# A two-layer retention and neighbourhood-attention transformer on one core: first stage with its loads put in another order, fewer unread products, and the decay tables and strips later

## The chip, the cores and the metric

One core of one Trainium2 chip. The core has TensorE (PE), VectorE (DVE), ScalarE (ACT), GpSimd (POOL) and SyncE (SP), and 16 DMA engines. Each engine works through its own row of instructions in order, and waits on semaphores for the others; DMAs are issued from the rows of SP, ACT and POOL. The metric is the device time of one execution in microseconds (us), lower is better; several runs are given by their median.

## The reference, cut to what matters

```python
for i in range(DEPTH):                       # 2 layers, D_MODEL 1024, 256 tokens x and 256 tokens ctx
    mod = (silu_c @ ada_w[i] + ada_b[i])[:, None, :]
    mod_c = silu_cc @ ada_w[i] + ada_b[i]
    sh1, sc1, g1, sh2, sc2, g2 = jnp.split(mod, 6, axis=-1)
    ...
    h = x * (1.0 + sc1) + sh1
    hc = ctx * (1.0 + sc1c) + sh1c
    if i % N_MIXERS == 0:
        y, yc = retention_mixer(h, hc, ret_w_in[j], ret_w_o[j], ret_decay[j], ang_row, ang_col, not last)
    else:
        y, yc = neighbourhood_mixer(h, hc, nat_w_in[j], nat_w_o[j], nat_rpb[j], not last)
    x = layer_norm(DN_ALPHA * x + g1 * y, ln_g[i, 0], ln_b[i, 0])
    h = x * (1.0 + sc2) + sh2
    x = layer_norm(DN_ALPHA * x + g2 * sq_relu_mlp(h, mlp_w1[i], mlp_w2[i]), ln_g[i, 1], ln_b[i, 1])
    ...                                      # ctx likewise, in the first layer
```

The retention layer projects `h @ w_in` to q, k, v and a gate for 4 heads, and weighs its scores with powers of a decay, `log_gamma = -exp(ret_decay)`, in both directions. All of it is float32.

## The kernel before, in words

Each float32 product is made of three products of a rounded format: every operand is split into a high part (a cast on ACT) and a low part (raw minus high, on DVE), and `mm3` adds high x high, high x low and low x high in PSUM. A weight therefore goes through a DMA into a raw tile, a cast `hi<-raw` and a subtraction `lo<-raw,hi` before TensorE reads it. Raw tiles come from a pool of four buffers, high and low parts from pools of five. Nearly every instruction has L89 as its line, since a helper issues it; tiles are told apart by name.

The change lies in the first stage (lines 888 to 953), which makes the modulation and the q and v projections of the first head. It goes in four quarters `i` of 256 of the 1024 rows that are contracted. A quarter needs

- its tokens: 256 columns of x and of ctx, one DMA each into `R` (`RR`)
- its columns of `ada_w`: four DMAs into `rawq`, in two pairs of arena slots used in turn (`AQ`)
- its rows of the q weights and the v weights: two DMAs into `raw`

and does the following. TensorE sums `ada_w` against silu(c) into `pada` (`quarter_sums`), turns the row of sums to columns (`quarter_columns`, `mod`), transposes two chunks of tokens (`chunk`, `pt`), and makes q products (`quarter_q`, into `pq`) and v products (`quarter_v`, into `pv`) of both chunks. ACT and DVE apply the modulation to one half of a chunk each (`aff<-pt,mod`), split the result (`hTh`, `hTl`), and split the weights. The sums, transposes and casts of quarter i+1 stand between the products of quarter i.

Ahead of the first useful product, and in gaps between the first sums, TensorE makes products of a constant tile, `still`, which nobody reads (`turn_over(n)`: n calls, each two instructions in the records). At the very end of the kernel it makes forty more, `px`, that nobody reads either.

The decays take a path of their own. `strip_tables` loads `lgn` (`ret_decay`) and a table of distances `dt`; ACT takes the exponential of `lgn`, POOL makes four more tables of `dt`. `make_strip(h)` makes the strip of head h of them: four exponentials on ACT and five operations on DVE. The masked scores read the strips later. `ln_rows` and `cst1` are other small loads of this stage.

In this stage the rows of PE, ACT and DVE hold the program's order (`on=True`), as SP's does throughout. Elsewhere a scheduler sets the order of those engines. After the stage, for head 0, the q's are rotated, v is evacuated, and `proj_T` makes k.

Of the kernel before, what the change touches and what calls it, by code (L numbers as in the profile page):

```python
# [10 lines left out]
F32 = mybir.dt.float32  # L11
F32R = mybir.dt.float32r
# [97 lines left out]
def kernel(  # L110
# [139 lines left out]
    units = []  # L250
    taken = [0]
    pending = []

# [18 lines left out]
    def load():  # L272

        src, k, ncol = specs[len(units)]
        raw = rawp.tile([P, k, ncol], F32, tag="raw", name=nm("raw"))
        sp.dma_start(out=raw[:], in_=src.rearrange("(k p) n -> p k n", p=P))
        hi = hip.tile([P, k, ncol], F32R, tag="hi", name=nm("hi"))
        lo = lop.tile([P, k, ncol], F32R, tag="lo", name=nm("lo"))
        units.append((hi, lo))

        def high(i):
            act.copy(out=hi[:, i], in_=raw[:, i])

        def low(i):
            dve.tensor_sub(out=lo[:, i], in0=raw[:, i], in1=hi[:, i].bitcast(F32))

        return high, low

# [18 lines left out]
    cst1 = cpool.tile([P, CONSTS.shape[1] - NC0], F32, tag="cst1", name="cst1")  # L307
    crow = scr("crow")[:, :P]
    sp.dma_start(out=crow[0:8, :], in_=c.rearrange("a (k p) -> (a k) p", p=P))
    act.dma_start(out=crow[8:16, :], in_=c_ctx.rearrange("(k p) -> k p", p=P))  # L310
    act.dma_start(out=crow[16:32, :], in_=ada_b[0][0 : 2 * D].rearrange("(r p) -> r p", p=P))
    act.dma_start(out=cst0[:], in_=consts[:, 0:NC0])

# [445 lines left out]
    def strip_tables():  # L759
# [7 lines left out]

        dt = slot(S_VL, [P, 5, 384], F32, "dt")
        sp.dma_start(out=dt[:, 0], in_=dist)
# [117 lines left out]

    quarter_x(0, act)
    raws = ada_quarter_load(0, AQ[0])
    wq_parts, wv_parts = load(), load()  # L890
    raws1 = quarter_loads(1)
    for e in (act, dve, pe):
        e.on = True
    pr = bank("pada")
    turn_over(3)
    first_columns()
    turn_over(4)
    quarter_sums(pr, raws, 0, range(0, 4))
    pts = [chunk_kinds(k) for k in range(2)]
    turn_over(1)  # L900
    quarter_sums(pr, raws, 0, range(4, KC))
    turn_over(2)
    quarter_sums(pr, raws, 1, range(0, 4))
    turn_over(2)
    quarter_sums(pr, raws, 1, range(4, KC))
    row = quarter_row(pr)
    turn_over(1)
    quarter_columns(pr, row, 0)
    turn_over(2)
    (qhigh, qlow), (vhigh, vlow) = wq_parts, wv_parts  # L910
    qhigh(0)
    modulate_kinds(0, pts[0], lambda: qlow(0))
    vhigh(0)
# [7 lines left out]
    pv = [bank("pv") for _ in range(4)]  # L921
    sp.dma_start(out=cst1[:], in_=consts[:, NC0:])

    for i in range(4):
        k = 2 * i
        wq, wv = take(2, 0)
        if i < 3:
            wq_parts, wv_parts = load(), load()
        if i == 0:
            rows = ln_rows()  # L930
            tabs = strip_tables()
        quarter_q(k, 0, wq)
        if i == 0:
            quarter_v(k, 0, wv)
            quarter_q(k + 1, 1, wq)
            quarter_v(k + 1, 1, wv, range(2))
        if i < 3:
            pr, row = quarter_rows(i + 1, raws)
        if i:
# [24 lines left out]
    act.on = dve.on = False  # L964
# [51 lines left out]
    for h in range(RH):  # L1016
# [3 lines left out]
        if h == 0:  # L1020
# [951 lines left out]
    flat = hTh[:].rearrange("p k t -> p (k t)")  # L1972
    px = bank("px")
    for d, m_, n_, far in (
        (0, P, 512, 0), (16, P, 512, 0), (32, P, 512, 0), (64, P, 512, 0), (112, P, 512, 0),
        (4, P, 512, 0), (0, 64, 512, 0), (0, P, 512, 1), (0, P, 256, 0), (64, P, 256, 0),
    ):
        src = hTl[:].rearrange("p k t -> p (k t)") if far else flat
        for _ in range(4):
            pe.matmul(  # L1980
                px[:m_, :n_], lhsT=src[:, 2048 + d : 2048 + d + m_], rhs=flat[:, :n_], start=True, stop=True
            )
    last_norm(0, 0, quarter(0), *m0)
# [49 lines left out]
```

## Time and profile before

| | |
|---|---|
| runs | 1236.78, 1232.69, 1232.66 us; median 1232.69 |
| profiled execution | 1234.7 us, its span 1232.9 us |
| mean granted clock of TensorE, profiled execution | 0.996 of full |
| busy: DVE, ACT, POOL | 811.1, 480.1, 170.8 us |
| moved by DMA | 194.30 MB, 158 GB/s over the span |
| first unread product | at 1.48 us |
| exponential of the decays | at 25.22 us |

A row of a timeline gives the start, the length, the engine, the operation with tile out<-in, and in brackets the idle time ahead of it on its engine with what released it. "hi<-raw" is a cast of weights, "lo<-raw,hi" the low part. A row of windows gives a stretch of the span, and for each engine how long it was busy with how many instructions, then the clock that TensorE was granted (1.00 is full) and the share and rate of the DMA engines.

### The profile page before, as it was taken

The numbers are of one execution on the slowest core, as the hardware profiler recorded it, in microseconds if no ns is written. First come the engines' busy times: TensorE is split into PE (matmuls) and PEld (weight loads), VectorE is DVE, ScalarE is ACT, GpSimd is POOL, SyncE is SP. The second block draws the span as 40 slices with busy tenths as digits, with TensorE's granted clock in tenths as the row PEclk, the third lists the DMA queues.
The fourth block names the chain that finished last, engine by engine and source line by source line (L and its number), as shares of the span: only waits on it lengthen the run. The fifth ranks groups of instructions, "written<-read, shape, count | busy, mean of one in ns | idle before, by whom it ended". The sixth has DMA issues, their size and how long they took to land.

```text
span 1232.9 us, 18106 instructions
## 1 busy us (share of the span) xinstructions
PE 1212.4 (98%) x7148; PEld 1013.4 (82%) x7148; DVE 811.1 (66%) x1265; ACT 480.1 (39%) x804; POOL 170.8 (14%) x203
## 2 busy tenths in 40 slices
PE   8999999999999999999999999999999989999999
PEld 6767788888888888888888888888887868999887
DVE  2598857777585476667766664467575677776445
ACT  2552221323223245442113341256465655565331
POOL 1103501420340140000120000231111100000002
PEclk9999999999999999999999999999999999999999
DMA  8756443375553224326656657335346543565660
GB/s 286 242 192 208 130 144 107 114 251 124 148 152 106 76 67 137 110 92 206 195 166 211 193 187 236 98 102 173 86 137 178 174 130 119 180 206 185 228 191 36
DMA packets 140213, 194.30 MB, mean 158 GB/s; under 512 B 22424, under 2 KB 83920, under 8 KB 140128
## 3 DMA queue, kind: packets, MB, share of 16 engines
q1 hardware_dynamic: 135328, 180.79, 47.1%
q0 software_dynamic: 3296, 9.49, 3.0%
q10 hardware_dynamic: 1504, 2.86, 0.7%
q8 instruction: 56, 0.92, 0.3%
q14 instruction: 29, 0.24, 0.1%
HBM read 188.28 MB, written 5.75 MB: 157 GB/s over the span
## 4 chain that ended last, share of the span: by engine, by line
PE 86%; DVE 5%; ACT 4%; DMA 3%; issue 2%; POOL 1%; SPq 0%; ACTq 0%; DVEq 0%; POOLq 0%
PE p L89 42%; PE pq L89 7%; PE pw L89 6%; PE pv L89 6%; PE pg L89 6%; PE pn L89 4%; PE pnv L89 3%; PE po L89 2%; PE pada L89 2%; ACT s L89 2%; DVE lo L89 1%; PE pS L89 1%; PE ppt L89 1%; PE pnw L89 1%; ACT hi L89 1%
## 5 line engine op out<-in xcount | busy, mean ns | idle before, releaser
L89 DVE TENSOR_TENSOR lo<-raw,hi 128x1024 fp32r<-128x1024 f32 (+1 forms) x235 | 277.5, 1192 | 162.4 <-ACT hi L89 162.0
L89 ACT CAST hi<-raw 128x1024 fp32r<-128x1024 f32 (+1 forms) x235 | 234.9, 1011 | 351.7 <-PE p L89 189.0
L89 PE MATMUL p<-hi,hid 128*128 128x512 f32 (+1 forms) x832 | 242.5, 374 | 0.0
L89 PEld LDWEIGHTS p<-hi,hid 128*128 128x128 f32 x832 | 152.2, 188 | 28.8 <-issue 1.2
L89 PE MATMUL p<-hTh,lo 128*128 128x256 f32 (+1 forms) x512 | 169.6, 331 | 0.8 <-DVE lo L89 0.8
L89 PE MATMUL p<-hTh,hi 128*128 128x256 f32 (+1 forms) x512 | 170.0, 332 | 0.0
L89 PE MATMUL p<-hTl,hi 128*128 128x256 f32 (+1 forms) x512 | 169.4, 331 | 0.0
L89 PE MATMUL p<-lo,hid 128*128 128x512 f32 (+1 forms) x416 | 155.4, 373 | 0.0
L89 POOL TENSOR_TENSOR R<-R,acc 128x512 f32<-128x512 f32 x40 | 66.8, 1680 | 299.1 <-DVE acc L89 299.1
L89 PEld LDWEIGHTS p<-hTh,lo 128*128 128x128 f32 x512 | 98.1, 192 | 9.8 <-DVE lo L89 1.0
L89 PEld LDWEIGHTS p<-hTh,hi 128*128 128x128 f32 x512 | 98.0, 192 | 9.5 <-issue 0.8
L89 PEld LDWEIGHTS p<-hTl,hi 128*128 128x128 f32 x512 | 98.1, 192 | 8.6
L89 DVE SCALAR_TENSOR_TENSOR acc<-rawa,scol,acc 128x1024 f32<-128x1024 f32 x49 | 62.2, 1282 | 42.9 <-DMA rawa<-in_ada_w_dram 42.8
L89 PEld LDWEIGHTS p<-lo,hid 128*128 128x128 f32 x416 | 78.4, 189 | 13.4
L89 DVE SCALAR_TENSOR_TENSOR strips<-rawa,scol,strips 128x512 f32<-128x512 f32 x84 | 70.1, 885 | 1.5 <-DMA rawa<-in_ada_w_dram 1.5
L89 ACT CAST hid<-r 128x256 fp32r<-128x256 f32 (+1 forms) x64 | 32.0, 500 | 82.7 <-DVE r L89 82.7
L89 ACT ACTIVATE s<-s,mn 128x512 f32<-128x512 f32 x64 | 45.5, 712 | 32.0 <-DVE mn L89 32.0
L89 DVE TENSOR_TENSOR hid<-r,hid 128x256 fp32r<-128x256 f32 (+1 forms) x64 | 34.6, 541 | 29.4 <-ACT hid L89 29.2
L89 PE MATMUL pw<-hi,oh 128*128 128x512 f32 x128 | 51.2, 400 | 0.0
L89 PE MATMUL pg<-hi,hTh 128*128 128x512 f32 x128 | 51.0, 398 | 0.0
L89 PE MATMUL pg<-lo,hTh 128*128 128x512 f32 x128 | 50.2, 392 | 0.4 <-DVE lo L89 0.4
L89 PE MATMUL pv<-hi,hTh 128*128 128x512 f32 x128 | 50.4, 394 | 0.0
(208 smaller groups left out, 2237.8 us busy)
## 6 DMA issues: line engine op xcount, KB each, us to landing
raw<-in_mlp_w_dram SPq DMA_DIRECT2D x128, 512.0 KB
rawa<-in_ada_w_dram SPq DMA_DIRECT2D x80, 512.0 KB
raw<-in_ret_w_in_dram SPq DMA_DIRECT2D x46, 512.0 KB
raw<-in_nat_w_in_dram SPq DMA_DIRECT2D x24, 512.0 KB
rawq<-in_ada_w_dram SPq DMA_DIRECT2D x16, 512.0 KB
raw<-in_ret_w_o_dram SPq DMA_DIRECT2D x16, 512.0 KB
bias<-rpb_rows POOLq DMA_DIRECT2D x16, 256.0 KB, 4.4
raw<-in_nat_w_o_dram SPq DMA_DIRECT2D x8, 512.0 KB
```

The lines of the kernel that those rows point to most:

```text
L89: r = f(*args, **kwargs)
```

## The change

- `load()` issues only the DMA; the high and low tiles are taken when the casts begin (`begin()`). All loads of quarters 0 and 1 are issued up front, those of quarter i+2 at the head of quarter i.
- The `ada_w` of quarter 0 is issued on SP ahead of quarter 0's tokens; these go from ACT's queue to SP's. The first constants go to the front of ACT's queue.
- `turn_over` goes from 15 calls (3, 4, 1, 2, 2, 1, 2) to 10 (5, 2, 1, 1, 1); the first two transposed chunks come behind the columns; the first cast of q weights stands in `modulate_kinds` between the two parts.
- `ln_rows`, `cst1` and `strip_tables` go from quarter 0 to quarter 1, behind the loads of quarter 3.
- `dt` goes from an arena slot to a tile of the constants' pool.
- The strips of heads 0 and 1 are made at the end of quarters 2 and 3, those of heads 2 and 3 after the first `proj_T`.
- The scaling of the residual `RR` by ALPHA, two DVE operations in quarter 3, becomes two ACT operations behind the first `proj_T` in the code; since ACT's order is the scheduler's there, it can put them where it finds room.
- The forty products `px` at the end are gone.

```diff
     def load():
-        src, k, ncol = specs[len(units)]
+        src, k, ncol = specs[loaded[0]]
+        loaded[0] += 1
         raw = rawp.tile([P, k, ncol], F32, tag="raw", name=nm("raw"))
         sp.dma_start(out=raw[:], in_=src.rearrange("(k p) n -> p k n", p=P))
-        hi = hip.tile([P, k, ncol], F32R, tag="hi", name=nm("hi"))
-        lo = lop.tile([P, k, ncol], F32R, tag="lo", name=nm("lo"))
-        units.append((hi, lo))
...
+        def begin():
+            hi = hip.tile([P, k, ncol], F32R, tag="hi", name=nm("hi"))
+            lo = lop.tile([P, k, ncol], F32R, tag="lo", name=nm("lo"))
+            units.append((hi, lo))
...
-        dt = slot(S_VL, [P, 5, 384], F32, "dt")
+        dt = cpool.tile([P, 2, D], F32, tag="G", name=nm("dt"))
+        dt = dt[:].rearrange("p a n -> p (a n)")[:, :1920].rearrange("p (k n) -> p k n", k=5)
...
-    quarter_x(0, act)
     raws = ada_quarter_load(0, AQ[0])
-    wq_parts, wv_parts = load(), load()
+    quarter_x(0, sp)
+    loads = [(load(), load())]
     raws1 = quarter_loads(1)
+    loads.append((load(), load()))
...
-    turn_over(3)
+    turn_over(5)
     first_columns()
-    turn_over(4)
-    quarter_sums(pr, raws, 0, range(0, 4))
-    pts = [chunk_kinds(k) for k in range(2)]
+    turn_over(2)
+    quarter_sums(pr, raws, 0, range(0, KC))
     turn_over(1)
-    quarter_sums(pr, raws, 0, range(4, KC))
-    turn_over(2)
     quarter_sums(pr, raws, 1, range(0, 4))
-    turn_over(2)
+    turn_over(1)
     quarter_sums(pr, raws, 1, range(4, KC))
     row = quarter_row(pr)
     turn_over(1)
     quarter_columns(pr, row, 0)
-    turn_over(2)
...
-    sp.dma_start(out=cst1[:], in_=consts[:, NC0:])
     for i in range(4):
         k = 2 * i
         wq, wv = take(2, 0)
+        if i < 2:
+            raws2 = quarter_loads(i + 2)
+            loads.append((load(), load()))
+        if i == 1:
+            rows = ln_rows()
+            sp.dma_start(out=cst1[:], in_=consts[:, NC0:])
+            tabs = strip_tables()
         if i < 3:
-            wq_parts, wv_parts = load(), load()
-        if i == 0:
-            rows = ln_rows()
-            tabs = strip_tables()
+            wq_parts, wv_parts = (f() for f in loads[i + 1])
...
-            if i < 2:
-                raws = quarter_loads(i + 2)
         else:
             ln_columns(rows)
             take(0, 3)
-            for a in range(2):
-                dve.tensor_scalar_mul(out=RR[a][:], in0=RR[a][:], scalar1=ALPHA)
...
-        for h in ((), (0,), (1,), (2, 3))[i]:
-            make_strip(h, *tabs)
+        if i > 1:
+            make_strip(i - 2, *tabs)
...
             proj_T(qkh[:, 2:4], qkl[:, 2:4], True)
+            for i in (2, 3):
+                make_strip(i, *tabs)
+            for a in range(2):
+                act.mul(out=RR[a][:], in_=RR[a][:], mul=ALPHA)
...
-    px = bank("px")
```

In the rows that follow, numbers behind a name only tell apart tiles of the same use.

On SP, before, the load of the decays `lgn` stands behind the constants and the q and v weights (`raw`) of quarter 1, and ahead of the loads of quarter 2:

```order
L89 DMA rawq_136<-in_ada_w_dram 128x4x256
L89 DMA rawq_137<-in_ada_w_dram 128x4x256
L89 DMA cst_82<-in_consts_dram 128x136
L89 DMA raw_239<-in_ret_w_in_dram 128x2x256
L89 DMA raw_243<-in_ret_w_in_dram 128x2x512
L89 DMA lgn<-in_ret_decay_dram 128x8
L89 DMA dt_255<-in_dist_dram 128x384
```

After, it stands behind the `ada_w` (`rawq_357`, `rawq_358`) and the weights of quarter 3:

```order
L89 DMA rawq_357<-in_ada_w_dram 128x4x256
L89 DMA rawq_358<-in_ada_w_dram 128x4x256
L89 DMA raw_363<-in_ret_w_in_dram 128x2x256
L89 DMA raw_365<-in_ret_w_in_dram 128x2x512
L89 DMA cst_82<-in_consts_dram 128x136
L89 DMA lgn<-in_ret_decay_dram 128x8
L89 DMA dt_376<-in_dist_dram 128x384
```

The load passes all the loads of quarters 2 and 3 on this queue.

On ACT, before, the exponential `lgn<-lgn` and its table load stand between the modulation of the first two chunks (`hTh`, `aff_225`) and that of chunk 2 (`aff_334`):

```order
L89 ACTIVATE hTh<-pt_171,mod_96 128x256
L89 ACTIVATE aff_225<-pt_172,mod_96 128x256
L89 CAST hi_132<-raw_130 128x512
L89 DMA rows_247<-in_ln_g_dram 32x128
L89 DMA rows_247<-in_ln_b_dram 32x128
L89 ACT_TABLE_LOAD
L89 ACTIVATE lgn<-lgn 128x8
L89 ACTIVATE aff_334<-pt_326,mod_96 128x256
L89 CAST hTh<-aff_334 128x512
L89 CAST hi_241<-raw_239 128x256 x2
```

After, they stand between the casts of quarter 1's v weights (`raw_140`) and the modulation of chunk 4 (`aff_447`), the first of quarter 2, whose q weights are `raw_245`:

```order
L89 ACTIVATE aff_346<-pt_341,mod_96 128x256
L89 CAST hTh<-aff_346 128x512
L89 CAST hi_251<-raw_140 128x512 x2
L89 DMA rows_367<-in_ln_g_dram 32x128
L89 DMA rows_367<-in_ln_b_dram 32x128
L89 ACT_TABLE_LOAD
L89 ACTIVATE lgn<-lgn 128x8
L89 ACTIVATE aff_447<-pt_439,mod_96 128x256
L89 CAST hTh<-aff_447 128x512
L89 CAST hi_382<-raw_245 128x256 x2
```

So the exponential has moved by one quarter, from ahead of chunk 2 to ahead of chunk 4.

On ACT, before, the last casts of the stage, those of quarter 3, follow one another with the modulation of chunks 6 and 7 between them:

```order
L89 ACTIVATE aff_571<-pt_563,mod_96 128x256
L89 CAST hTh<-aff_571 128x512
L89 CAST hi_504<-raw_502 128x256 x2
L89 ACTIVATE aff_591<-pt_586,mod_96 128x256
L89 CAST hTh<-aff_591 128x512
L89 CAST hi_508<-raw_506 128x512 x2
L89 ACTIVATE e_612<-dt_255,lgn 128x384
```

After, the two scalings of the residual, `R_100` (x) and `R_101` (ctx), stand among them:

```order
L89 ACTIVATE aff_553<-pt_545,mod_96 128x256
L89 CAST hTh<-aff_553 128x512
L89 CAST hi_488<-raw_363 128x256 x2
L89 ACTIVATE R_100<-R_100 128x2048
L89 ACTIVATE aff_573<-pt_568,mod_96 128x256
L89 ACTIVATE R_101<-R_101 128x2048
L89 CAST hTh<-aff_573 128x512
L89 CAST hi_490<-raw_365 128x512 x2
L89 ACTIVATE e_594<-dt_376,lgn 128x384
```

Both have moved ahead of the cast of chunk 7 and of quarter 3's v weights (`raw_365`).

More of the change, by code (lines that the diff above doesn't have):

```diff
@@ L251 @@
     taken = [0]
+    loaded = [0]
     pending = []
@@ L272, in load, with high, low @@
     def load():
-        src, k, ncol = specs[len(units)]
+        src, k, ncol = specs[loaded[0]]
+        loaded[0] += 1
         raw = rawp.tile([P, k, ncol], F32, tag="raw", name=nm("raw"))
         sp.dma_start(out=raw[:], in_=src.rearrange("(k p) n -> p k n", p=P))
-        hi = hip.tile([P, k, ncol], F32R, tag="hi", name=nm("hi"))
-        lo = lop.tile([P, k, ncol], F32R, tag="lo", name=nm("lo"))
-        units.append((hi, lo))
[L281 to L287, printed above, removed]
+        def begin():
+            hi = hip.tile([P, k, ncol], F32R, tag="hi", name=nm("hi"))
+            lo = lop.tile([P, k, ncol], F32R, tag="lo", name=nm("lo"))
+            units.append((hi, lo))
+            def high(i):
+                act.copy(out=hi[:, i], in_=raw[:, i])
+            def low(i):
+                dve.tensor_sub(out=lo[:, i], in0=raw[:, i], in1=hi[:, i].bitcast(F32))
+            return high, low
+        return begin
     def lows(n=100):
@@ L308 @@
     crow = scr("crow")[:, :P]
+    act.dma_start(out=cst0[:], in_=consts[:, 0:NC0])
     sp.dma_start(out=crow[0:8, :], in_=c.rearrange("a (k p) -> (a k) p", p=P))
@@ L311 @@
     act.dma_start(out=crow[16:32, :], in_=ada_b[0][0 : 2 * D].rearrange("(r p) -> r p", p=P))
-    act.dma_start(out=cst0[:], in_=consts[:, 0:NC0])
     def cv(name, p0=0, p1=P):
@@ L908 @@
     quarter_columns(pr, row, 0)
-    turn_over(2)
-    (qhigh, qlow), (vhigh, vlow) = wq_parts, wv_parts
-    qhigh(0)
-    modulate_kinds(0, pts[0], lambda: qlow(0))
+    pts = [chunk_kinds(k) for k in range(2)]
+    (qhigh, qlow), (vhigh, vlow) = (f() for f in loads[0])
+    modulate_kinds(0, pts[0], lambda: (qhigh(0), qlow(0)))
     vhigh(0)
@@ L938 @@
             pr, row = quarter_rows(i + 1, raws)
+            raws = raws2
         if i:
@@ L1971 @@
             mm2b(1, 1, u, held[2 * (u - 14) + 1], i)
-    flat = hTh[:].rearrange("p k t -> p (k t)")
-    px = bank("px")
[L1974 to L1982, printed above, removed]
     last_norm(0, 0, quarter(0), *m0)
```

## The prediction

> **What bounds the kernel now.** I read the page first. Its first line gives the span, its second the busy time of each engine, and the chain that ended last names who sets the end.
>
> ```profile
> span 1232.9 us, 18106 instructions
> PE 1212.4 (98%) x7148; PEld 1013.4 (82%) x7148; DVE 811.1 (66%) x1265; ACT 480.1 (39%) x804; POOL 170.8 (14%) x203
> PE 86%; DVE 5%; ACT 4%; DMA 3%; issue 2%; POOL 1%; SPq 0%; ACTq 0%; DVEq 0%; POOLq 0%
> ```
>
> TensorE is busy 98% of the span, so a stage can get faster only where TensorE does work that nobody reads or waits, and any new wait of TensorE counts in full. Next I read the timeline of TensorE through the first stage and into the next; columns are start, busy time of the row, engine, operation, tile out<-in, and in brackets the idle time ahead with its releaser.
>
> ```profile
> 1.48 2.93 PE L89 MATMUL pq<-still 128*128 128x256 f32 x6 [1.48 <-DVE still L89]
> 18.58 0.70 PE L89 MATMUL pq<-hTh,hi 128*128 128x512 f32 x2
> 35.64 0.64 PE L89 MATMUL pada<-rawq,cT 128*32 128x128 f32 x16 [0.46 <-DMA rawq<-in_ada_w_dram]
> 44.58 0.62 PE L89 MATMUL pq<-hTh,hi 128*128 128x512 f32 x2
> 48.26 0.40 PE L89 MATMUL pv<-lo,hTh 128*128 128x512 f32 x1
> 58.30 0.50 PE L89 MATMUL pv<-lo,hTh 128*128 128x512 f32 x1 [0.31 <-DVE lo L89]
> 80.12 0.50 PE L89 MATMUL pg<-lo,hTh 128*128 128x512 f32 x1 [0.45 <-DVE lo L89]
> 81.58 0.64 PE L89 MATMUL pada<-rawa,cT 128*32 128x256 f32 x8 [0.49 <-DMA rawa<-in_ada_w_dram]
> ```
>
> The first product that counts starts at 18.58. The later waits are under 0.5 us each: the front costs time, the rest of the stage almost none. What feeds the stage is in the windows; columns are the window, its length, busy time of PE, PEld, DVE, ACT and POOL with instruction counts, granted clock, DMA share and GB/s.
>
> ```profile
> 0.00:4.00 4.00, 2.52 (x6) 1.85 (x6) 0.54 (x2) 0.53 (x1) 0.41 (x6) 1.00 0.35 97
> 4.00:20.00 16.00, 13.19 (x106) 8.78 (x105) 3.10 (x11) 3.37 (x8) 0.00 (x0) 1.00 1.10 356
> 20.00:30.00 10.00, 9.92 (x102) 8.06 (x103) 4.18 (x10) 2.94 (x5) 4.18 (x3) 1.00 0.78 244
> 30.00:45.00 15.00, 14.00 (x122) 10.80 (x121) 6.70 (x15) 6.75 (x14) 2.68 (x5) 1.00 1.07 351
> ```
>
> The DMA engines run at about 350 GB/s, except in the ten microseconds from 20, where loads wait for their issue. What they carry, from the DMA issues of the first 45 us:
>
> ```profile
> rawq<-in_ada_w_dram SPq DMA_DIRECT2D x16, 512.0 KB
> raw<-in_ret_w_in_dram SPq DMA_DIRECT2D x4, 256.0 KB
> raw<-in_ret_w_in_dram SPq DMA_DIRECT2D x5, 512.0 KB
> R<-in_x_dram SPq DMA_DIRECT2D x3, 256.0 KB
> R<-in_ctx_dram SPq DMA_DIRECT2D x3, 256.0 KB
> ```
>
> A quarter is two token loads (0.524 MB), four ada loads (2.097) and two weight loads (0.262 and 0.524): 3.41 MB. The two pieces of the constants are 0.07 MB each by their shapes.
>
> **The change part by part.** *Front and loads (gain).* Five of 15 unread calls go, and ada precedes the tokens. What ends the front afterwards is one quarter with one constants piece, or 3.48 MB: an estimate at 356 GB/s from zero is 9.8 us, and with a landing lag of some 2 to 2.7 (below) and two casts about 13, against 18.58. That lead of some 5 us isn't kept whole, because ada of quarter 2 comes next. Before, 6.97 MB (two quarters, constants) plus the 0.20 of the distance table and 2.62 of tokens and ada stand ahead of the sums at 35.64: 9.79 MB. By 30 us some 8.5 MB had moved (the first three windows: 0.39, 5.70 and 2.44). The other 1.3 MB at 351 take 3.6 us: 33.6, so landing lags by 2.0. After, 9.53 MB stand there; the loads are issued as slots come free, so the rate can stay at 351: 20 + (9.53 - 6.1)/0.351 = 29.8, landed at 31.8. That is 3.8 us earlier. TensorE would then reach the product of quarter 2, now at 44.58, at about 40.7.
>
> *The decay load (loss).* The load of the decays goes on SP from behind quarter 1 to behind quarter 3. ScalarE's row is in program order, so its exp on that load stands ahead of the modulation and casts of chunk 4.
>
> ```profile
> 18.55 0.34 SPq L89 DMA_DIRECT2D lgn<-in_ret_decay_dram  x1
> 25.22 0.21 ACT L89 ACTIVATE lgn<-lgn 128x8 f32<-128x8 f32 x1 [1.67 <-DMA lgn<-in_ret_decay_dram]
> 40.94 0.56 ACT L89 ACTIVATE aff<-pt,mod 128x256 f32<-128x256 f32 x1 [5.38 <-DVE aff L89]
> 42.06 0.71 ACT L89 CAST hi<-raw 128x256 fp32r<-128x256 f32 x2
> 45.90 1.29 DVE L89 TENSOR_TENSOR lo<-raw,hi 128x512 fp32r<-128x512 f32 x2
> ```
>
> Before, the exp waits 1.67 us at 25.22, when ScalarE has little to do. Its 6.97 MB are through at 20 + 0.87/0.351 = 22.5, a lag of 2.7. After, four quarters and both constants, 13.8 MB, are ahead of it: 20 + 7.7/0.351 = 42.0, and with lags of 2.0 to 2.7 it lands at 44.0 to 44.7; I take 44.3. The exp ends 0.2 later. From modulation (40.94) to the first cast of quarter 2's q weights (half of the 0.71 from 42.06) are 1.5 us: its product starts at 46.0, 1.4 after 44.58. TensorE, there at 40.7, idles 5.3 us. From modulation to the first low part of the v weights (45.90 plus half of 1.29) are 5.6 us, so the second v product comes at 50.1 instead of 48.26: **+1.9** (1.6 to 2.3). This holds gain and loss together: the lead is spent waiting. The queue behind the exp is ScalarE's modulation, high parts and, through them, VectorE's low parts; TensorE waits for all.
>
> *Clock after that gap.* Two places of the trace show what follows idle time, each as a window and the next:
>
> ```profile
> 467.50:470.95 3.45, 1.44 (x10) 1.15 (x10) 1.21 (x3) 3.13 (x5) 0.00 (x0) 1.00 0.08 25
> 470.95:474.37 3.42, 3.31 (x15) 3.31 (x16) 3.24 (x8) 2.80 (x6) 0.00 (x0) 0.50 0.52 153
> 1010.26:1013.67 3.41, 0.58 (x26) 0.31 (x15) 1.92 (x6) 3.34 (x9) 0.00 (x0) 1.00 0.19 67
> 1013.67:1017.08 3.41, 3.41 (x40) 2.93 (x41) 3.01 (x6) 0.62 (x2) 0.00 (x0) 0.50 0.02 5
> ```
>
> A window with 2.0 of 3.45 us idle is followed by 3.4 us at half clock, and so is one with 2.8 idle. So 5.3 us idle brings at least one such stretch: 1.7 us of work lost, of which some 0.5 lies beside the wait for low parts: **+1.2** (0 to 2.9: none that shows, or two stretches with the same cover).
>
> *Scaling the residual (loss).* It leaves VectorE's row of quarter 3 for ScalarE's, as two instructions of 128x2048. They stand between the casts of quarter 3's q weights and its v weights, on both sides of the modulation of chunk 7. No ScalarE row has that size; the nearest are:
>
> ```profile
> 55.70 0.56 ACT L89 ACTIVATE aff<-pt,mod 128x256 f32<-128x256 f32 x1 [1.27 <-DVE aff L89]
> L89 ACT CAST hi<-raw 128x1024 fp32r<-128x1024 f32 x217 | 226.3, 1051 | 346.5 <-PE p L89 189.0 <-PE pg L89 49.7 <-PE pw L89 41.6
> L89 ACT CAST hi<-raw 128x512 fp32r<-128x512 f32 x10 | 5.8, 616 | 0.0
> L89 ACT ACTIVATE xn<-R,nmr,rstd 128x1024 f32<-128x1024 f32 x4 | 5.0, 1245 | 8.2 <-DVE nmr L89 8.2
> ```
>
> From 616 to 1051 ns for 512 columns more, another 1024 columns make 1.92 us. Twice 1051 or 1245 give 2.10 and 2.49. I take 1.92, since a longer instruction pays its start once: 3.84 for both, of which the 1.27 idle ahead of 55.70 takes part. The rest, 2.6, pushes the casts of the v weights, and TensorE already waits 0.31 for their low part at 58.30: **+2.6** (2.5 to 3.7). A gap of that length again precedes half clock in the rows above, but with its own low parts late behind it: **+1.0** (0 to 1.7).
>
> *VectorE (gain).* Two strips of five operations and the scaling leave its row.
>
> ```profile
> 64.88 1.22 DVE L89 TENSOR_SCALAR R<-R 128x2048 f32<-128x2048 f32 x1
> ```
>
> Two of 1.22 and ten strip operations come later or go; only the small waits at 80.12 and 81.58 can shrink: **-0.5** (0 to -0.9). The strips come after the first k projection, beside TensorE's work.
>
> *The unread products at the end.*
>
> ```profile
> 1223.65 5.40 SPq L89 DMA_DIRECT2D out_dram<-xn  x5
> 1227.51 1.55 SPq L89 DMA_DIRECT2D out_dram<-xn  x3
> 1229.01 1.11 PE L89 MATMUL px<-hTh 128*128 128x256 f32 x8
> ```
>
> TensorE's unread products end at 1230.1, the issue of the stores at 1229.1, and the span at 1232.9; the stores' landing sets the end, so: **0** (0 to -0.5, if the products delayed the stores' issue at all; the difference of their ends, 1.0, bounds it, and I take half). Of the rest, the first constants on ScalarE's queue and the transposes behind the columns cost nothing, as the bytes of quarter 0 set the front. The distance table comes on SP right behind the decays, and GpSimd makes four tables of it:
>
> ```profile
> L89 POOL TENSOR_SCALAR dt<-dt 128x384 f32<-128x384 f32 x4 | 5.7, 1435 | 24.9 <-DMA dt<-in_dist_dram 24.7
> ```
>
> From about 45 they take until 51. The first strip stands in ScalarE's row behind the v casts of quarter 3, later than 56, so that is hidden; nothing else waits on GpSimd there.
>
> *Sum.* 1.9 + 1.2 + 2.6 + 1.0 - 0.5 + 0 = +6.2. The profiled execution took 1234.7 us, 1.8 over its span; the median of the runs shown is 1232.69, so the sum gives 1240.9 on the profiled execution and **1238.9** on the median. The bounds of the sum are 1.6 + 0 + 2.5 + 0 - 1.4 = +2.7 and 2.3 + 2.9 + 3.7 + 1.7 = +10.6. As the ends are hardly met together, I take half the distance to each: 1237.1 to 1241.1 is the forecast's own range.
>
> [...] In the trace 2.0 and 2.8 us of idle time within one window of 3.4 us were enough for a half-clock window. [...]
>
> **The rivals.** Half a per cent, about what a measurement of this kernel can tell from no change, is 6.2 us: faster is below 1226.5, slower above 1238.9.
>
> *Only the long gap drops the clock* (0.16). The gap of 2.6 us is a wait between products, not a whole idle window: v's first product, q's two low products and others lie within it. For it: 2.6 us spread over two windows leaves each over half busy. Against: 467.50 has 1.44 of 3.45 us busy and was followed by half clock. The sum loses 1.0: 1237.9. [...]
>
> *The decay load lands in time* (0.14; no change). If the loads of quarter 3 run ahead, or the small load overtakes larger ones on free DMA engines, the exp has its data by 40.7 and the lead isn't spent: -3.8 in place of +1.9 and +1.2, with 2.6 + 1.0 - 0.5 left, -0.7: 1232.0. It decides at one number, the landing at 40.7 or before. Against: 7.7 MB from 20 at 351 GB/s takes until 42.0 without any lag, so the rate would have to be 373 GB/s or more. For: the window from 4 to 20 had 356 with a slow start in front.
>
> *The scaling hides too* (0.06). If, besides, ScalarE reaches it earlier, as its lead grows with TensorE's, 3.6 of loss go: -4.3, 1228.4. Against: TensorE already waits at 58.30 with only 1.27 idle on ScalarE ahead.
>
> *Nothing drops the clock* (0.04): 1.9 + 2.6 - 0.5 = +4.0, 1236.7.
>
> *Two cold stretches* (0.10; slower). If the idle of 5.3 us fills one window and spoils the next, a second stretch of 3.4 us at half clock follows; it decides when 3.4 us of the gap lie in one window and some 1.9 in the next, since 2.0 idle were enough at 467.50. The clock then costs 2.9 rather than 1.2: +7.9, 1240.6; with the scaling and the second clock term at their upper ends, 1242.4.
>
> **How the numbers follow.** The forecast, 1238.9, has 0.50. The bound of slower lies on it; its own bounds reach a little farther up than down, so I give 0.28 to slower and 0.22 to same. With the two cold stretches, 0.10, slower is 0.38. Faster needs more than -6.2, which only the far end of the hidden case has: 0.03. Same has the rest: 0.22 + 0.16 + 0.14 + 0.03 + 0.04 = 0.59. The range runs from 1231.5, just below the case in which the decay load lands in time, to 1242.5, the upper end of the two cold stretches; it leaves out the hidden case (0.06), the few hundredths above, and some 0.05 below 1231.5 of the case at 1232.0, less than two in ten.
>
> **What would show it.** Right: the product of quarter 2's q starts at 46.0, with an idle time of about 5 us in front whose releaser is ScalarE's cast, and on ScalarE the exp of the decays starts at about 44.3, released by the load. The first q product is at 13 to 14. A window with clock 0.50 behind the gap. ScalarE's row has two instructions of about 1.9 us ahead of the last v casts, and TensorE waits 2 to 3 us for the low part there. The last store lands as late after TensorE's last read product as before. Wrong: the exp is released before 41, or TensorE has no wait behind it; the two scaling instructions lie in idle time of ScalarE; TensorE is busy from 14 to 60; or the front is still at 18, in which case the unread products were not what paced it, and the time would be about 4 us longer than I say.

## The result, and the profile after

The changed kernel takes 1236.72 us (median of 12 runs, 1235.92 to 1238.83); the kernel before, run beside it, 1233.28 (12 runs, 1231.51 to 1236.78). The ratio is 1.003, with a 95% interval of 1.0021 to 1.0039: slower by 3.4 us, less than half a per cent. The forecast was 6.2 us more, 1238.9, with a range of 1231.5 to 1242.5. The two losses in the stage came as forecast; most of what was missed lies behind it.

The page of the changed kernel: span, busy times, chain that ended last.

```profile
span 1234.5 us, 18012 instructions
PE 1203.7 (98%) x7098; PEld 1005.1 (81%) x7098; DVE 808.5 (65%) x1263; ACT 482.3 (39%) x806; POOL 171.1 (14%) x203
PE 87%; DVE 5%; ACT 4%; DMA 2%; issue 1%; SPq 0%; DVEq 0%; ACTq 0%
```

TensorE is busy 8.7 us less (50 instructions fewer), and the span is 1.6 longer. About 8.5 of the 8.7 are the forty products at the end, which in before run from 1221.59 to 1230.1 beside the last stores; the products saved in the front are eaten again by waits and half clock. Where, is in TensorE's timeline:

```profile
12.83 0.74 PE L89 MATMUL pq<-hTh,hi 128*128 128x512 f32 x2 [0.29 <-ACT hi L89]
30.12 0.64 PE L89 MATMUL pada<-rawq,cT 128*32 128x128 f32 x16 [0.86 <-DMA rawq<-in_ada_w_dram]
31.61 0.65 PE L89 MATMUL pada<-rawq,cT 128*32 128x128 f32 x16 [0.84 <-DMA rawq<-in_ada_w_dram]
45.85 1.11 PE L89 MATMUL pq<-hTh,hi 128*128 128x512 f32 x2 [3.61 <-ACT hi L89]
51.36 0.39 PE L89 MATMUL pv<-lo,hTh 128*128 128x512 f32 x1
62.70 0.50 PE L89 MATMUL pv<-hi,hTh 128*128 128x512 f32 x1 [1.81 <-ACT hi L89]
63.51 0.79 PE L89 MATMUL pv<-lo,hTh 128*128 128x512 f32 x1 [0.31 <-DVE lo L89]
```

The first q product is at 12.83 instead of 18.58. Then come three places with waits, for the `ada_w` of quarter 2, for ScalarE at 45.85, and for ScalarE at 62.70. ScalarE's timeline has the causes of the last two:

```profile
44.19 0.21 ACT L89 ACTIVATE lgn<-lgn 128x8 f32<-128x8 f32 x1 [12.86 <-DMA lgn<-in_ret_decay_dram]
...
57.46 1.91 ACT L89 ACTIVATE R<-R 128x2048 f32<-128x2048 f32 x1
59.28 0.54 ACT L89 ACTIVATE aff<-pt,mod 128x256 f32<-128x256 f32 x1
59.72 1.90 ACT L89 ACTIVATE R<-R 128x2048 f32<-128x2048 f32 x1
```

ScalarE stands still for 12.86 us ahead of the exponential of the decays, and the two scalings leave it no idle time at 59.28. Each of the three places is followed by half clock; here are the stretches around them, in pairs (window, length, busy of PE, PEld, DVE, ACT, POOL, granted clock, DMA share, GB/s):

```profile
28.94:32.35 3.41, 1.70 (x45) 0.97 (x38) 1.92 (x4) 2.37 (x4) 0.00 (x0) 1.00 1.08 362
32.35:35.76 3.41, 3.41 (x9) 2.63 (x10) 0.40 (x1) 0.00 (x0) 0.00 (x0) 0.50 1.10 347
42.59:46.00 3.41, 0.14 (x1) 0.15 (x2) 0.47 (x1) 1.78 (x5) 1.31 (x2) 1.00 0.13 46
46.00:49.41 3.41, 3.41 (x18) 1.87 (x22) 2.13 (x5) 1.80 (x5) 3.29 (x3) 0.50 0.25 78
59.65:63.07 3.42, 1.61 (x7) 0.88 (x5) 0.91 (x2) 3.42 (x5) 0.00 (x0) 1.00 0.44 144
63.07:66.48 3.41, 3.10 (x8) 2.39 (x8) 3.31 (x7) 3.41 (x7) 0.00 (x0) 0.50 0.35 93
```

Follow one product through both traces, and the gap between its two starts gives the account of the stage: the changed kernel is 5.5 us ahead at 28, 2.5 ahead at 37 (the two waits, 1.5 net, and 1.5 of half clock), 3.1 behind at 51 (a step of 5.6), 6.6 behind at 67 (3.4 more). Then, where the forecast gave back 0.5, it gets back 3.5: it is 4.9 behind at 99 and 3.0 at 127. Here are two of the products followed, each in before and then in the changed kernel:

```profile
60.48 0.39 PE L89 MATMUL pv<-lo,hTh 128*128 128x512 f32 x1
67.04 0.39 PE L89 MATMUL pv<-lo,hTh 128*128 128x512 f32 x1
124.01 0.47 PE L89 MATMUL pw<-hi,oh 128*128 128x512 f32 x1
127.02 0.47 PE L89 MATMUL pw<-hi,oh 128*128 128x512 f32 x1
```

By the end of the products that count it is 1.7 behind. Most of the last 1.3 is the half-clock stretch that before has at 470.95 and this execution happens to miss.

The end itself is as forecast: the issue of the stores starts 2.1 us behind the last product that counts, as it did before (1223.65 against 1221.5).

```profile
1223.17 0.28 PE L89 MATMUL p<-hi,hid 128*128 128x256 f32 x1
...
1225.30 5.36 SPq L89 DMA_DIRECT2D out_dram<-xn  x5
```

### The profile page after: what moved, and what is told of

Same layout as the page of the kernel before. It is cut to its first block, busy times and chain, and to the rows that moved or that the text cites. A ratio compares the mean times of both kernels' runs of the same rounds, so it can differ in the third digit from the quotient of the medians.

```text
span 1234.5 us, 18012 instructions
## 1 busy us (share of the span) xinstructions
PE 1203.7 (98%) x7098; PEld 1005.1 (81%) x7098; DVE 808.5 (65%) x1263; ACT 482.3 (39%) x806; POOL 171.1 (14%) x203
## 4 chain that ended last, share of the span: by engine, by line
PE 87%; DVE 5%; ACT 4%; DMA 2%; issue 1%; SPq 0%; DVEq 0%; ACTq 0%
PE p L89 41%; PE pg L89 7%; PE pq L89 7%; PE pw L89 7%; PE pv L89 6%; PE pn L89 4%; PE pnv L89 3%; PE po L89 3%; PE pada L89 2%; ACT s L89 2%; PE pS L89 1%; DVE lo L89 1%; PE ppt L89 1%; PE pnw L89 1%; ACT hi L89 1%
## 5 line engine op out<-in xcount | busy, mean ns | idle before, releaser
L89 PE MATMUL pq<-hTh,hi 128*128 128x512 f32 x128 | 49.6, 398 | 4.4 <-ACT hi L89 4.4
L89 PE MATMUL pv<-lo,hTh 128*128 128x512 f32 x128 | 51.3, 401 | 0.3 <-DVE lo L89 0.3
```

What stands on the lines that cost most here:

```text
L89: r = f(*args, **kwargs)
```

## The experiments

Twelve kernels, each timed beside the kernel before, whose median was 1232.8 to 1233.3 in every batch. The theory behind the prediction: the lead of the front is lost at the exponential of the decays, then ScalarE's scalings cost more. Against it stood that the loads set the end of the stage whatever is done, and that the scaling is hidden.

**The decays loaded early.** Undone: the place of the small loads and the exponential.

```diff
+        if i == 0:
+            rows = ln_rows()
+            sp.dma_start(out=cst1[:], in_=consts[:, NC0:])
+            tabs = strip_tables()
         if i < 2:
             raws2 = quarter_loads(i + 2)
...
-        if i == 1:
-            rows = ln_rows()
-            sp.dma_start(out=cst1[:], in_=consts[:, NC0:])
-            tabs = strip_tables()
```

> The changed kernel with one thing undone: the loads of the decays, distances, second constants and norm rows stand at the head of quarter 0 again, ahead of the loads of quarter 2. Theory A (the decay load on ScalarE's row is the largest loss): in the changed kernel TensorE was 2.5 us ahead of before when it ran into the 3.61 us wait at 45.85 and was 3.1 behind after it and its half-clock stretch, a step of 5.6. That step goes. The 0.27 MB now ahead of quarter 2 cost 0.8 us of lead at 350 GB/s, and the exponential may hold the modulation of chunk 2 by 0.5: about 1236.7 - 5.6 + 1.3 = 1232.4. Theory B (the loads of the stage set its end, so the lead cannot be kept and the wait only moves to the loads of quarter 3): a wait of 2 to 4 us on a load or a cast between 43 and 50, 1235 to 1236.7.

Measured: 1232.26 us (0.9996 of before, 0.9985 to 1.0007), 4.5 less than the changed kernel. The wait at 45 is gone. But in this trace the lead is lost earlier, at the `ada_w` of quarter 2:

```profile
34.40 1.08 PE L89 MATMUL pada<-rawq,cT 128*32 128x128 f32 x16 [2.26 <-DMA rawq<-in_ada_w_dram]
```

The last `ada_w` of quarter 2 is there at 34.4 instead of 31.6, for 0.27 MB at the 351 GB/s of before that would be 0.8 us. Part of the rest may be time of SP: in before, which also has the small loads ahead of those of quarter 2, SP's row waits 2.2 us for the norm rows to land, ahead of the load of the distances, and issues the tokens of quarter 2 at 22.82, against 16.62 in the changed kernel. TensorE is at 0.50 of its clock from 33.58 to 40.40, and the product of quarter 2 starts at 46.04, no earlier than in the changed kernel; the profiled execution took 2.0 us more than the median. So the sum of 1.3 for this cost was too low, the agreement of 1232.26 with 1232.4 is in part luck, and this run doesn't decide between the theories. The run below with only the two loads moved does.

**The scaling back on VectorE**, and **both undone** (the edit above and this one).

```diff
             take(0, 3)
+            for a in range(2):
+                dve.tensor_scalar_mul(out=RR[a][:], in0=RR[a][:], scalar1=ALPHA)
...
-            for a in range(2):
-                act.mul(out=RR[a][:], in_=RR[a][:], mul=ALPHA)
```

> The changed kernel with one thing undone: the residual's scaling is on VectorE in quarter 3 again, where before had it. Theory A (the two scalings on ScalarE push the last casts): the waits of 1.81 and 0.31 us at 62.70 and the half-clock stretch behind them go, a step of 3.4: 1233.3. Theory B (VectorE needs its 2.4 us there, and the small waits around 80 come back): 0.9 of it is given back, 1234.2. Theory C (the late v weights of quarter 3, not the scaling, make that wait): no change, 1236.7.

> Both undone: the decay load early and the scaling on VectorE. If the two losses are separate (theory A) the sum of the single effects holds: 1236.7 - 4.3 - 3.4 = 1229.0, that is 4.3 us faster than before. If they draw on the same slack, or the loads set the end of the stage (theory B), it is at 1232 to 1233.

Measured: 1236.8 and 1233.19 us (1.003, 1.002 to 1.004; 0.9993, 0.9979 to 1.0007). Each is no better than its neighbour with the scaling on ScalarE, 1236.72 and 1232.26. Yet the wait of 1.81 at 62.70 is gone, and no half clock follows there. With the scaling on VectorE, TensorE waits later:

```profile
122.95 0.50 PE L89 MATMUL pw<-hi,ol 128*128 128x512 f32 x1 [1.14 <-DVE ol L89]
127.15 0.66 PE L89 MATMUL pT<-cst,gs 128*128 128x128 f32 x4 [1.66 <-POOL gs L89]
```

The changed kernel has neither wait. The kernel before has the second:

```profile
123.60 0.66 PE L89 MATMUL pT<-cst,gs 128*128 128x128 f32 x4 [1.66 <-POOL gs L89]
```

VectorE's row differs there. It has background operations in it, `strips<-rawa,scol,strips`, which work on `ada_w` for a later modulation; their raw tiles `rawa` come from the same four buffers as `raw`. With the scaling on VectorE, four of them stand in one piece ahead of the low parts:

```profile
117.29 2.74 DVE L89 SCALAR_TENSOR_TENSOR strips<-rawa,scol,strips 128x512 f32<-128x512 f32 x4
```

In the changed kernel it is one:

```profile
117.60 0.72 DVE L89 SCALAR_TENSOR_TENSOR strips<-rawa,scol,strips 128x512 f32<-128x512 f32 x1
```

The scheduler has put the work of head 0 in another order, 50 us after the edit. The four in one piece aren't needed for the second wait: the kernel before has it too, with one operation. What differs from the changed kernel there is the place of that last operation against TensorE's row. Its end frees the buffer for the next load of output weights, and ScalarE's cast of them stands ahead of its `sg`, from which GpSimd makes `gs`. Before:

```profile
115.45 0.74 DVE L89 SCALAR_TENSOR_TENSOR strips<-rawa,scol,strips 128x512 f32<-128x512 f32 x1
116.22 0.37 SPq L89 DMA_DIRECT2D raw<-in_ret_w_o_dram  x1
119.06 0.39 PE L89 MATMUL pw<-hi,oh 128*128 128x512 f32 x1
120.11 1.05 ACT L89 CAST hi<-raw 128x1024 fp32r<-128x1024 f32 x1 [4.79 <-DMA raw<-in_ret_w_o_dram]
```

After:

```profile
118.34 0.37 SPq L89 DMA_DIRECT2D raw<-in_ret_w_o_dram  x1
121.97 1.05 ACT L89 CAST hi<-raw 128x1024 fp32r<-128x1024 f32 x1 [1.83 <-DMA raw<-in_ret_w_o_dram]
123.94 0.39 PE L89 MATMUL pw<-hi,oh 128*128 128x512 f32 x1
```

In all fourteen traces the first `gs` behind this load is done 7.0 to 7.3 us after its issue. TensorE reaches the transposition of `gs` 2.7 us after its first `pw` product if nothing holds it. Before, the load is issued 2.8 us ahead of that product, so TensorE comes too early; after, it is issued 5.6 ahead, and TensorE comes late enough. So the question was whether this order or the time at which TensorE arrives in the span makes the waits; three runs below answer it.

**Fifteen unread calls again.**

```diff
     first_columns()
-    turn_over(2)
+    turn_over(4)
     quarter_sums(pr, raws, 0, range(0, KC))
-    turn_over(1)
+    turn_over(2)
     quarter_sums(pr, raws, 1, range(0, 4))
-    turn_over(1)
+    turn_over(3)
```

> The changed kernel with 15 unread calls as before had (four more in the first sums, one more behind them); everything else as changed. Theory A (the front's lead is spent ahead of the exponential of the decays, whose time the loads set): the front is 1.5 to 2.5 us later, the waits for the ada_w of quarter 2 shrink, the product of quarter 2 starts at 45.9 as it did, and the time is 1236.7 within 0.7. Theory B (the front's time goes through to the end): 1238.5.

Measured: 1236.41 us, within 0.3 of the changed kernel. The waits for `ada_w` are gone, and the product of quarter 2 waits for ScalarE all the same and starts within 0.5 us:

```profile
45.33 0.73 PE L89 MATMUL pq<-hTh,hi 128*128 128x512 f32 x2 [3.97 <-ACT hi L89]
```

Five calls taken out or left in make no difference to the whole as long as the exponential waits for its load. In the front they do: the first q product comes 2.7 us later than with ten.

```profile
15.52 0.73 PE L89 MATMUL pq<-hTh,hi 128*128 128x512 f32 x2 [0.29 <-ACT hi L89]
```

**Only the two loads moved**: their issue goes behind quarter 2's loads, the exponential stays.

```diff
             loads.append((load(), load()))
+        if i == 0:
+            dt = strip_loads()
         if i == 1:
             rows = ln_rows()
             sp.dma_start(out=cst1[:], in_=consts[:, NC0:])
-            tabs = strip_tables()
+            tabs = strip_tables(dt)
```

> The changed kernel with only the issue of two loads moved: the decays and the distances are loaded behind quarter 2's loads instead of quarter 3's; the exponential stays where the changed kernel has it, ahead of chunk 4's modulation. 10.5 MB are ahead of it: 20 + 4.4/0.351 + 2 to 2.7 = 34.5 to 35.2, long before ScalarE needs it at 42. Theory A (the wait for this load is the loss): the 3.61 us wait and the half-clock stretch behind it go, a step of 5.6, and the waits for quarter 2's ada_w stay as in the changed kernel: 1236.7 - 5.6 = 1231.1. Theory B (the loads of quarter 3 take the wait's place): 1234 or more.

Measured: 1228.93 us (0.9976, 0.9965 to 0.9986), 7.8 less than the changed kernel and faster than before. ScalarE has the data at 33.72 and keeps its order. In TensorE's timeline there is one wait for the `ada_w` of quarter 2, none at 45, and the scaling's:

```profile
31.24 0.64 PE L89 MATMUL pada<-rawq,cT 128*32 128x128 f32 x16 [0.86 <-DMA rawq<-in_ada_w_dram]
55.37 0.50 PE L89 MATMUL pv<-hi,hTh 128*128 128x512 f32 x1 [1.81 <-ACT hi L89]
```

The gain beyond 5.6 fits the wait and the half clock around 32 that are missing in this execution, about 2.3 us, though one profile can't show that for all runs.

**`ada_w` ahead of the tokens in every quarter**, on top of that.

```diff
     def quarter_loads(i):
-        quarter_x(i, sp)
-        return ada_quarter_load(i, AQ[i % 2])
+        raws = ada_quarter_load(i, AQ[i % 2])
+        quarter_x(i, sp)
+        return raws
```

> As the run with the two loads moved, and with the ada_w of every quarter issued ahead of its tokens instead of only quarter 0's. The ada_w of quarter 2 then lands 1.5 us earlier (0.52 MB at 351 GB/s). Theory A (the two waits of 0.85 us for it, and the half clock behind them, cost 3.0): 1.5 of the waits go, and with them the clock stretch of 1.5: 1231.1 - 3.0 = 1228.1. Theory B (clock as by longer gaps only, or the next load is late instead): 1.5 at most, 1229.6 to 1231.

Measured: 1227.55 us (0.9957, 0.9945 to 0.997), 1.4 less. A wait of 0.85 for `ada_w` stays, and ends at 30.81 instead of 31.24, so the load is 0.4 us earlier there and not 1.5. With the half clock already missing in the run before, only the smaller expectation could be met.

**The scaling on GpSimd**, on top of that.

```diff
+            for a in range(2):
+                pool.tensor_scalar_mul(out=RR[a][:], in0=RR[a][:], scalar1=ALPHA)
...
-                act.mul(out=RR[a][:], in_=RR[a][:], mul=ALPHA)
```

> As the run before, with the residual's scaling on GpSimd in quarter 3 instead of ScalarE. GpSimd has nothing else from 54 to 100, and the order of VectorE's row later on is that of the changed kernel, not that of the run with the scaling on VectorE. Theory A (the scaling on ScalarE costs 3.4 in the stage, and what came back with it on VectorE was VectorE's other order around 120): the full 3.4 is gained, 1228.1 - 3.4 = 1224.7. Theory B (what came back then comes back wherever the scaling goes, as TensorE only reaches the later waits sooner): 1228.

Measured: 1231.53 us, 4.0 more than without; both theories missed it. VectorE's timeline in this run, with GpSimd's row first:

```profile
48.38 10.72 POOL L89 TENSOR_SCALAR R<-R 128x2048 f32<-128x2048 f32 x2 [6.10 <-PE pt L89]
```

```profile
48.71 3.86 DVE L89 TENSOR_TENSOR hTl<-aff,hTh 128x512 fp32r<-128x512 f32 x1 [1.35 <-ACT hTh L89]
...
53.16 0.53 DVE L89 TENSOR_SCALAR aff<-pt,mod 128x256 f32<-128x256 f32 x1
54.98 2.94 DVE L89 TENSOR_TENSOR hTl<-aff,hTh 128x512 fp32r<-128x512 f32 x1 [1.28 <-ACT hTh L89]
```

The same operation takes 0.69 in the run before:

```profile
48.97 0.69 DVE L89 TENSOR_TENSOR hTl<-aff,hTh 128x512 fp32r<-128x512 f32 x1 [1.34 <-ACT hTh L89]
```

GpSimd was idle and still not free to use: VectorE's operation `hTl<-aff,hTh`, on two tiles, takes 2.2 to 3.2 us longer beside GpSimd's, 3.86 and 2.94 against 0.69, and TensorE waits 1.24 and 2.26 us for low parts. What holds it up is not shown, and not every operation of two tiles is held up: `lo<-raw,hi` right behind takes its usual 0.75 for two from 52.49 on, and 1.28 for two from 57.84 on (0.75 and 1.29 in the run before), while GpSimd's two operations are recorded as running from 48.38 to 59.10.

**Before without the unread products at its end.** Removed: the loop over `px`.

```diff
-    px = bank("px")
...
-            pe.matmul(
-                px[:m_, :n_], lhsT=src[:, 2048 + d : 2048 + d + m_], rhs=flat[:, :n_], start=True, stop=True
-            )
```

> The kernel before without the forty unread products at its end; they write nothing that is read, so the output is whole. By the prediction 0 (to -0.5): 1232.5 to 1233.0. Rival: they kept the clock or the last stores from slowing, and leaving them out costs 0.5 to 1.

Measured: 1232.94 us, ratio 1.0001 (0.9992 to 1.0011): nothing, as forecast.

**The scaling held back on ScalarE**, on top of the run with `ada_w` first, and, in a second kernel, in the changed kernel itself.

```diff
             pg = gate(1)
+            act.on = True
             act.activation(out=gs[:, 1, :], in_=pg[:], func=AF.Silu)
+            for a in range(2):
+                act.mul(out=RR[a][:], in_=RR[a][:], mul=ALPHA)
+            act.on = False
...
-            for a in range(2):
-                act.mul(out=RR[a][:], in_=RR[a][:], mul=ALPHA)
```

> As the run with ada_w first, and with the residual's scaling kept on ScalarE but held, in the written order, behind the gate of the first head, where ScalarE is idle for some 10 us (95.7 to 105.9 in that run). VectorE's row around 115 to 125 is the changed kernel's. Theory A (the scaling in the stage costs what the stage shows, 2.1 there without a half-clock stretch, up to 3.4 with one): 1227.55 - 2.1 to 3.4 = 1224.2 to 1225.5. Theory B (whatever is won there is lost again at the waits around 120): 1227.5.

> The changed kernel with one thing changed: the residual's scaling held behind the gate of the first head on ScalarE. Theory A (the prediction's step on the scaling, 3.6, is right, and the run with the scaling on VectorE gave it back by another order of VectorE's row around 120): 1236.7 - 3.4 = 1233.3. Theory B: 1236.7, as in that run.

Measured: 1223.41 us (0.9921, 0.9907 to 0.9935) and 1232.87 (1.0002, 0.9993 to 1.0011), 4.1 and 3.9 less than without. In the first, ScalarE scales in its idle time, and TensorE's wait for the v weights is down to that of before:

```profile
92.82 3.71 ACT L89 ACTIVATE R<-R 128x2048 f32<-128x2048 f32 x2
```

```profile
52.67 0.50 PE L89 MATMUL pv<-lo,hTh 128*128 128x512 f32 x1 [0.28 <-DVE lo L89]
```

Neither kernel has a wait between 115 and 130. TensorE comes to that place earlier than in the kernel before and in the run with the scaling on VectorE, and the waits don't come back: they belong to the order. In the two kernels the load of the output weights is issued 4.0 and 5.7 us ahead of the first `pw` product, against 2.8 in before and 1.0 with the scaling on VectorE. 1223.41 is the fastest of all kernels here, 9.7 us less than before and 13.3 less than the changed kernel.

**Before with only the strips put off.** The distances go to the constants' pool as well.

```diff
-        for h in ((), (0,), (1,), (2, 3))[i]:
-            make_strip(h, *tabs)
+        if i > 1:
+            make_strip(i - 2, *tabs)
...
             proj_T(qkh[:, 2:4], qkl[:, 2:4], True)
+            for i in (2, 3):
+                make_strip(i, *tabs)
```

> The kernel before with only the strips put off as in the change (heads 0 and 1 at the end of quarters 2 and 3, heads 2 and 3 behind the k projection) and the distances in the constants' pool, which the later reads ask for. The scaling stays on VectorE. By the prediction 0 to -0.9. Theory A: VectorE's row around 120 is now that of the run with the scaling on VectorE, with four background operations ahead of the low parts, so it shows the waits of 1.1 and 1.7 there: -0.9 + 1.6 to 2.7, that is 1233.5 to 1234.6. Theory B (these waits hang on the time at which TensorE comes, not on the order): 1232 to 1232.8.

Measured: 1234.91 us (1.0019, 1.001 to 1.0028), 1.8 more than before. The waits are there, and so are the four operations in VectorE's row:

```profile
120.38 0.50 PE L89 MATMUL pw<-hi,ol 128*128 128x512 f32 x1 [1.00 <-DVE ol L89]
124.75 0.66 PE L89 MATMUL pT<-cst,gs 128*128 128x128 f32 x4 [1.80 <-POOL gs L89]
```

```profile
114.72 2.73 DVE L89 SCALAR_TENSOR_TENSOR strips<-rawa,scol,strips 128x512 f32<-128x512 f32 x4
```

So the strips put off come with the bad order where the scaling is on VectorE, and with the good one in the kernels run here that have it on ScalarE, early or late, or on GpSimd. Without the scaling moved, they cost 1.8 us where the prediction had a small gain. What makes the scheduler choose so was not tried.

**Before with ten unread calls.** The seven counts are 3, 2, 0, 2, 1, 1, 1 instead of 3, 4, 1, 2, 2, 1, 2.

> The kernel before with 10 unread calls instead of 15, and nothing else changed. The first useful product comes earlier by up to 1.9 (ten instructions of 0.37). Theory A (the lead is bounded by the landing of quarter 2's ada_w at 35.6, where TensorE already waits 0.46): no gain, 1232.3 to 1232.8, with the wait at 35.6 longer by what the front gains. Theory B (the front goes through): 1231.

Measured: 1233.49 us, ratio 1.0006 (0.9994 to 1.0019): no gain. The trace is a poor witness of the reason. The first q product comes at 18.23, only 0.35 earlier, since the front ran slower in this execution: its eight transposes take 2.31 us from 10.17 on, against 1.09 before. At the sums of quarter 2 that lead is gone, and TensorE waits longer all the same, since two parts of this `ada_w` are there at least 1.1 and 1.5 us later than in the trace of before, where the same sums start at 34.56 and 35.64:

```profile
35.69 0.64 PE L89 MATMUL pada<-rawq,cT 128*32 128x128 f32 x16 [0.86 <-DMA rawq<-in_ada_w_dram]
37.15 1.08 PE L89 MATMUL pada<-rawq,cT 128*32 128x128 f32 x16 [0.82 <-DMA rawq<-in_ada_w_dram]
```

The medians show that fewer unread products alone bring nothing. That the loads bound the lead, as expected, is not shown by this trace.

## Why the prediction was right, and where it was not

- *Front.* Forecast at 13 to 14, found at 12.83. The prediction has the bytes of quarter 0 end it. With ten calls that is nearly so: two other traces with this front (only the two loads moved, and the changed kernel with the scaling held back) show TensorE waiting 0.23 and 0.20 us at about 10.1 for the last `ada_w` of quarter 0. But the changed kernel itself waits for no load there, and with fifteen calls the front is at 15.52, without a wait for `ada_w`. So the calls are 2.7 of the lead of 5.8, and that ten of them just fit beside the bytes is luck, as the prediction doesn't add up TensorE's row.
- *`ada_w` of quarter 2.* Forecast to land at 31.8; its last products start at 31.61. But TensorE was forecast at the product of quarter 2 at 40.7 and was there at 42.2 (45.85 less 3.61). The step failed by a term: the prediction had no half clock behind these waits.
- *Decay load.* The exponential was forecast at 44.3, the product at 46.0, the loss with its clock at 3.1; found were 44.19, 45.85, and 51.36 against 48.26, which is 3.1. The idle time is 3.61 and not 5.3, since TensorE came later. The end of it was right because the load sets that time and not TensorE's arrival; the run with fifteen calls shows it, and the one with only the two loads moved shows that the wait is the loss.
- *Scaling.* Forecast 1.92 us each, found 1.91 and 1.90; forecast a step of 3.6 with its clock, found 3.4, and 3.9 and 4.1 when it is held back. TensorE waits for the high part of the v weights (1.81) more than for the low part (0.31), which changes nothing.
- *VectorE.* This is the term that was wrong in size: forecast -0.5 (to -0.9), found -3.5 in the trace. Its reason doesn't hold alone either: with only the strips put off the time rose by 1.8. The waits at 80.12 and 81.58 did go, 0.9 together. The wait of 1.66 at 123.60 in the trace of before went too; the prediction never priced it, as it looked at the rows to 82 only and took the order behind the stage for unchanged. It went because the last background operation ahead of it ends earlier against TensorE's row, and with it the load that it holds back. Held against the kernels whose order differs, that order is worth about what the scaling in the stage costs: with the scaling on VectorE, the change would have had neither. About 0.9 of the 3.5 is not assigned to a wait.
- *End.* Forecast 0, found 0 with only the unread products removed.
- *Rivals.* That the load lands by itself in time fell with 44.19. That only the long gap drops the clock fell with three stretches at half clock. The row of 467.50, 1.44 of 3.45 us busy and 0.50 of the clock behind it, told what came: windows with 1.70 and 1.61 busy were followed by the same (more on this at the end).

In sum, the two losses came as forecast, 3.1 + 3.4 for 3.1 + 3.6, and the gain behind the stage was 3 us larger than forecast. That takes the forecast of 6.2 to 3.0 in the traces, near the 3.4 that the medians show. The total is just below the forecast's own range (1237.1 to 1241.1), and inside the stated one, which was drawn wider for other cases than this.

## What to carry to other kernels

A small load that an engine waits for in program order cost here what stood ahead of it on its queue, not its own size: the decays, 4 KB, brought TensorE a wait of 3.61 us and a step of 5.6, and with their issue moved ahead of quarter 3's loads the kernel took 7.8 us less. Issue such a load early, and leave the instruction that reads it where it is. Time won in front was only kept as far as each later load came earlier too (of 5.5 us at 28, 2.5 were left at 37, behind two waits for `ada_w`), so add up the bytes ahead of each wait before taking filler work away. Where a scheduler orders the rest, compare its whole order after an edit, since waits may come or go far behind the place of the edit, here 50 us. Background work that read from the same buffers as the later loads held a load back until it ended (at 116.19 in before and 118.32 in the changed kernel, the issue at 116.22 and 118.34), so its place counts even where its engine is not the bottleneck.

## What the runs showed of the hardware

Half clock followed windows that were not wholly idle. The windows of 3.41 us in which TensorE was busy 1.61 and 1.70 us were followed by 0.50 of the clock (above); so was one with 1.75 in the run of before with ten calls. In the changed kernel with the scaling held back, the same place as 28.94 above had 1.91 us busy and kept its clock:

```profile
28.94:32.35 3.41, 1.91 (x53) 1.18 (x44) 1.96 (x4) 2.61 (x4) 0.00 (x0) 1.00 1.08 361
32.35:35.76 3.41, 3.41 (x20) 2.86 (x19) 0.36 (x1) 0.00 (x0) 0.00 (x0) 1.00 1.11 348
```

In the traces of before and of the changed kernel the stretches at half clock start whole numbers of 3.41 us apart: at 470.95, 1013.67 and 1034.15, and at 32.35, 46.00, 63.07, 1015.39 and 1035.87. In windows cut on these starts, up to the last product that counts, the changed kernel lost its clock behind the five with 0.14 to 1.70 us busy, and kept it behind all with 1.90 and more. Before lost it behind three, with 0.58, 1.44 and 1.58, and kept it behind all with 2.47 and more; it also kept it behind one at the head of the span, 3.33 to 6.74, with 1.07. So the border lay near half of the window here, and it is not sharp by this measure: the run with the decays loaded early has 1.75 busy from 57.47 to 60.88 and keeps its clock, as much as the run of before with ten calls had where it lost it.

The starts of the changed kernel lie 1.7 us off a whole number of windows from those of before. That like waits end differently for this reason is the author's estimate: the same wait of 1.8 us was followed by a stretch here (59.65 above) and in the run with only the two loads moved (0.50 of the clock from 56.75 to 60.16, behind a window with 1.29 busy), and by none in two others, that with the decays loaded early and that with `ada_w` first. The latter:

```profile
53.61:57.02 3.41, 2.02 (x8) 1.42 (x9) 2.83 (x5) 3.41 (x8) 0.00 (x0) 1.00 0.01 2
57.02:60.43 3.41, 3.41 (x15) 2.50 (x14) 3.24 (x6) 3.41 (x5) 0.00 (x0) 1.00 0.50 159
```

That fits a spread between executions of one kernel, 2.9 us among the twelve of the changed kernel.
